# A hybrid diffusion backbone on one core: the framework's timeline simulation as the scheduling model of every engine's queue

## The chip, the core and the metric

The kernel runs on one core of one Trainium2 chip. A core has a matrix engine (TensorE, "PE" in the profile), a vector engine (VectorE, "DVE"), a scalar engine (ScalarE, "ACT"), a general engine (GpSimd, "POOL") and a queue engine that only issues transfers (SyncE, "SP"). Each takes its instructions from a queue of its own, in the order in which they stand there, and waits at the head of the queue until the semaphores that the instruction needs have come. TensorE writes to PSUM, eight banks; the other memory on the chip is SBUF. The metric is the device time of one execution in microseconds (us); smaller is better. A figure given for a kernel is the median of its runs.

## The reference

Two layers work on 256 context tokens and 512 latent tokens of width 1024. Each layer is a mixer and an MLP, both between norms and with modulation from a conditioning vector (adaLN). Cut to what matters:

```python
def token_mixer(h_lat, h_ctx, p, rope, layer_idx, ctx_out):
    a_l, b_l, c_l, d_l, gate_l = split_cols(h_lat @ p['w_in'], GROUP_COLS)
    a_x, b_x, c_x, d_x, gate_x = split_cols(h_ctx @ p['w_in'], GROUP_COLS)
    ya = diff_attention(a_l, a_x, ...)       # softmax minus lambda * softmax
    yb = rwkv7_time_mix(b_l, b_x, ...)       # a recurrence in both directions
    yc = retention(c_l, c_x, ...)            # decayed linear attention, both directions
    yd = window_gqa(d_l, d_x, ...)           # banded attention with sink logits
    m = sum(sigmoid(gate_n) * (y_n @ w_branch[n]) for the four branches)
    return m @ p['w_out']

def sq_relu_mlp(h, w_up, w_down):
    return jnp.square(jax.nn.relu(h @ w_up)) @ w_down
```

All of it is float32. The output is the latent stream after two layers, (1, 512, 1024).

## The kernel before

The kernel is written against a framework that takes a program of tiles and builds the engines' queues from it. `kernel` opens a `TileContext` (line 1825), and `Build.run` states the whole computation inside it, layer by layer. When the context closes, the framework orders every engine's queue, gives out the buffers of the pools, and adds the semaphores. To order the queues it walks a simulated machine: whenever an engine is free in it, the first instruction in the program's order whose inputs and buffers are ready there goes next into that engine's queue. So the final order follows the program's order, with exchanges between neighbours where the simulated machine has something later ready sooner. The framework has two such machines, and the kernel before uses its default one.

Products are made in pieces of 128 by 128 weights against 256 or 512 tokens. A product of full precision is three matmuls: `mm3` (line 398 issues them) multiplies the high part of one operand with the high and low parts of the other, and the low with the high. So each block of weights is loaded (`unit`, line 262, on SyncE's queue, into four raw buffers), cast to its high part (line 265, ScalarE, `wh`), and its low part is the difference (line 266, `wl`, on VectorE, or on GpSimd where `pool_split` says so), in four buffers of each. The activations are kept as `hh` and `hl`.

The stages of a layer, in the order of the program:

- `branch_b` (line 802), the recurrence, as blocks of 64 tokens. Its chain goes from engine to engine: a norm of the keys (`head_sums`, line 594; a power operation on GpSimd, line 856; `rb`, line 619, a copy on VectorE that spreads the result over columns; the transposes `prs`, line 625, on TensorE), gram matrices (`pgr`, line 1001, masked into `gb` and `gk` by VectorE), a triangular inverse of 31 steps of two VectorE operations (lines 1123 and 1125), then small products (`pq`, `pz`, `ppu`, `pst`).
- The rest of the mixer: `branch_a` (scores `pas`), `branch_c` (`pcy`), `branch_d`, with the rotation of queries and keys in `spill` (`prot`, line 483); `gates` and `lift`, which bring the branches together.
- The output projection (`pwo`), the residual and the norm (`norm_tile`; a power operation on GpSimd, line 358; `xn`, line 377; the transposes `pnt`, line 381).
- The MLP (`pm` for the hidden layer, `pd` for the output).

While a branch's chain has TensorE wait, other projections fill it. The program says so by hand: `fill` (line 452) takes a number of microseconds of matmuls from a list of generators (`filler`) and states them there. The numbers stand in the table `FILL` (line 27), two sets, one for each layer. The modulations of later norms (`ada_steps`, `pada`, line 291) are such fillers too.

## Time and profile before

| | us |
|---|---|
| median of three runs | 2775.91 |
| lowest and highest run | 2770.07 and 2776.38 |
| the profiled execution | 2782.34 |
| its span, first to last instruction | 2780.6 |

| engine | busy us | share of the span |
|---|---|---|
| PE | 2623.3 | 94% |
| DVE | 1492.3 | 54% |
| ACT | 1082.6 | 39% |
| POOL | 703.2 | 25% |

The profile is of one execution. Busy time counts the instructions at work; the matmuls of a queue overlap, so a busy PE needn't be at its peak. The granted clock is the share of TensorE's full clock in a stretch. A wait is idle time of an engine, put down to what came last before the engine went on. Times in a view are microseconds from the first instruction, unless marked ns.

### The profile page before, as it was taken

The page shows a single profiled execution, that of the slowest core. Times are in us where ns is not written, and L with a number is a line of the kernel's source. Part 1 is how long each engine was busy: PE and PEld are TensorE (multiplying, and loading weights), DVE is VectorE, ACT ScalarE, POOL GpSimd, SP SyncE. Part 2 cuts the span into 40 slices and gives each one's busy share as a digit, 9 for nine tenths or more (in the row PEclk, how much of TensorE's full clock was granted, in tenths as well). Part 3 has the DMA queues.
Part 4 walks back from the last instruction along what each step waited for, and adds up shares of the span by engine and source line. Part 5 has one row for each costly group of instructions (what it writes and reads, how often), then busy time and mean ns, then how long its engine had stood idle before and what let it go on. Part 6 is the DMA issues. An engine that isn't in the chain of part 4 may idle for free.

```text
span 2780.6 us, 44114 instructions
## 1 busy us (share of the span) xinstructions
PE 2623.3 (94%) x17093; PEld 2095.9 (75%) x17093; DVE 1492.3 (54%) x2521; ACT 1082.6 (39%) x2144; POOL 703.2 (25%) x774
## 2 busy tenths in 40 slices
PE   7899899999999999999999988989999999999998
PEld 4766677887788778887888776667788686778886
DVE  5676752775745452333334569585385864433444
ACT  4432442563446333222223344244364463333332
POOL 2434342113330321101101344353322422201011
PEclk9999999999999999999999989899999999999999
DMA  6133545444433522322222222354644536342322
GB/s 237 58 117 106 170 154 161 120 126 156 157 122 109 168 92 93 108 91 90 86 94 86 93 67 73 105 194 159 189 130 153 185 106 201 116 135 95 95 95 91
DMA packets 177777, 346.51 MB, mean 125 GB/s; under 512 B 19440, under 2 KB 33312, under 8 KB 177568
## 3 DMA queue, kind: packets, MB, share of 16 engines
q1 hardware_dynamic: 139680, 279.99, 31.0%
q10 hardware_dynamic: 30208, 44.97, 4.6%
q0 software_dynamic: 7680, 18.75, 2.6%
q8 instruction: 134, 2.20, 0.3%
q14 instruction: 75, 0.61, 0.1%
HBM read 280.55 MB, written 63.08 MB: 124 GB/s over the span
## 4 chain that ended last, share of the span: by engine, by line
PE 72%; DVE 13%; DMA 4%; ACT 4%; issue 4%; POOL 4%; SPq 0%; ACTq 0%; DVEq 0%; POOLq 0%
PE pm L398 39%; PE pd L398 14%; PE pwo L398 4%; PE plift L398 2%; PE pada L291 1%; DVE xm L1125 1%; DVE tmp L1123 1%; PE pas L1335 1%; PE pay L579 1%; DVE cpl L557 1%; DMA wr<-w_in 1%; DMA wr<-w_out 1%; PE pq L1158 1%; PE pst L1236 1%; POOL wl L266 1%
## 5 line engine op out<-in xcount | busy, mean ns | idle before, releaser
L398 PE MATMUL pm<-hh,wh 128*128 128x512 f32 (+1 forms) x2272 | 832.3, 366 | 9.4 <-ACT wh L265 3.9
L398 PE MATMUL pm<-hh,wl 128*128 128x512 f32 (+1 forms) x2272 | 822.0, 362 | 11.4 <-POOL wl L266 11.1
L398 PE MATMUL pm<-hl,wh 128*128 128x512 f32 (+1 forms) x2272 | 820.7, 361 | 0.5 <-DVE hl L393 0.4
L265 ACT CAST wh<-wr 128x512 fp32r<-128x512 f32 x516 | 317.9, 619 | 687.7 <-PE pm L398 281.6
L266 DVE TENSOR_TENSOR wl<-wr,wh 128x512 fp32r<-128x512 f32 x364 | 261.7, 722 | 498.5 <-ACT wh L265 477.6
L398 PEld LDWEIGHTS pm<-hh,wh 128*128 128x128 f32 x2272 | 438.4, 193 | 97.3 <-issue 25.1
L398 PEld LDWEIGHTS pm<-hh,wl 128*128 128x128 f32 x2272 | 438.4, 193 | 79.5 <-POOL wl L266 13.1
L398 PEld LDWEIGHTS pm<-hl,wh 128*128 128x128 f32 x2272 | 438.7, 193 | 68.9 <-issue 8.8
L266 POOL TENSOR_TENSOR wl<-wr,wh 128x512 fp32r<-128x512 f32 x152 | 210.3, 1387 | 424.2 <-ACT wh L265 392.3
L1738 POOL TENSOR_TENSOR s<-r 128x256 f32<-128x256 f32 (+1 forms) x98 | 91.3, 931 | 758.8 <-ACT r L1737 754.4
L398 PE MATMUL pd<-wh,sh 128*128 128x512 f32 x640 | 254.6, 399 | 3.2 <-DVE hf L385 2.4
L398 PE MATMUL pd<-wh,sl 128*128 128x512 f32 x640 | 252.6, 396 | 1.1 <-DVE sl L1740 1.0
L398 PE MATMUL pd<-wl,sh 128*128 128x512 f32 x640 | 253.3, 396 | 0.0
L1740 DVE TENSOR_TENSOR sl<-s,sh 128x256 fp32r<-128x256 f32 (+1 forms) x98 | 58.0, 592 | 177.4 <-POOL s L1738 177.4
L398 PEld LDWEIGHTS pd<-wh,sh 128*128 128x128 f32 x640 | 120.7, 189 | 37.7 <-DVE hf L385 3.1
L398 PEld LDWEIGHTS pd<-wh,sl 128*128 128x128 f32 x640 | 120.6, 188 | 30.6 <-DVE sl L1740 1.9
L398 PEld LDWEIGHTS pd<-wl,sh 128*128 128x128 f32 x640 | 120.7, 189 | 28.3 <-DVE wl L266 0.2
L1784 DVE TENSOR_TENSOR acc<-acc,pd 128x512 f32<-128x512 f32 x120 | 82.4, 686 | 50.5 <-PE pd L398 49.4
L1525 POOL TENSOR_TENSOR merged<-merged,gateb 128x256 f32<-128x256 f32 (+1 forms) x72 | 88.3, 1232 | 78.3 <-DVE gateb L1524 77.6
L1737 ACT ACTIVATE r<-pm 128x256 f32<-128x256 f32 (+1 forms) x98 | 50.6, 516 | 118.7 <-PE pm L398 118.6
L398 PE MATMUL plift<-yh,wh 128*128 128x256 f32 (+1 forms) x192 | 73.3, 382 | 9.2 <-DVE gateb L1524 3.7
L1339 ACT ACTIVATE ae<-pas,asum 128x768 f32<-128x768 f32 (+1 forms) x80 | 65.2, 818 | 34.0 <-DVE asum L1337 31.4
(388 smaller groups left out, 3990.0 us busy)
## 6 DMA issues: line engine op xcount, KB each, us to landing
wr<-w_in SPq DMA_DIRECT2D x228, 256.0 KB
wr<-ada SPq DMA_DIRECT2D x192, 256.0 KB
wr<-w_up SPq DMA_DIRECT2D x128, 256.0 KB
wr<-w_down SPq DMA_DIRECT2D x128, 256.0 KB
graw<-gate ACTq DMA_DIRECT2D x64, 256.0 KB
x<-x SPq DMA_DIRECT2D x28, 512.0 KB
gateb<-graw SPq DMA_DIRECT2D x32, 384.0 KB
wr<-w_br SPq DMA_DIRECT2D x32, 256.0 KB
```

The source lines that it names most:

```text
L265: nc.scalar.copy(hi, raw)
L266: (nc.gpsimd if self.pool_split > h else nc.vector).tensor_tensor(lo, raw, f32(hi), ALU.subtract)
L291: nc.tensor.matmul(ps[32 * j:32 * j + 32, 0:256], self.silu[:, k, :], raw[:, i * 256:(i + 1) * 256], start=k % kn == 0, stop=k % kn == kn ...
L398: self.nc.tensor.matmul(ps, a[u], b[v], start=start and i == 0, stop=stop and i == 2)
L557: self.nc.vector.tensor_tensor(lo, src, f32(hi), ALU.subtract)
L579: self.nc.tensor.matmul(py, v.rearrange("p e d -> p (e d)"), w[i], start=start and i == 0, stop=stop and i == 1)
L1339: nc.scalar.activation(e[:, 0:nkc], ps[:, 0:nkc], ACTF.Exp, bias=sums[:, c:c + 1], accum_out=sums[:, 2 + c:3 + c])
L1525: nc.gpsimd.tensor_tensor(mo, mo, t, ALU.add)
L1737: nc.scalar.activation(r[:, 0:n], ps[:, 0:n], ACTF.Relu)
L1738: nc.gpsimd.tensor_tensor(s2[:, 0:n], r[:, 0:n], r[:, 0:n], ALU.mult)
L1740: nc.vector.tensor_tensor(s[1][:, o:o + n], s2[:, 0:n], f32(s[0][:, o:o + n]), ALU.subtract)
L1784: nc.vector.tensor_tensor(a, a, po[t - t0], ALU.add)
```

## The change

The `TileContext` is opened with the flag that makes the framework walk its other machine, the timeline simulation, when it orders the queues. The program that is stated inside the context is the same, and so are the engine, the operands and the pools of every instruction, and the `FILL` numbers. All five queues are ordered anew, SyncE's loads among them, and so the semaphores differ too.

```diff
     out = nc.dram_tensor("out", (SEQ, D), F32, kind="ExternalOutput").ap()
-    with tile.TileContext(nc) as tc:
+    with tile.TileContext(nc, schedule_with_timeline_sim=True) as tc:
         Build(tc, aps, out).run()
```

## Rows read from the trace of the kernel before

**Rows 1.** The page's first part: busy us, share of the span, instructions of each engine.
```profile
PE 2623.3 (94%) x17093; PEld 2095.9 (75%) x17093; DVE 1492.3 (54%) x2521; ACT 1082.6 (39%) x2144; POOL 703.2 (25%) x774
```

**Rows 2.** Busy us by stage, columns named in the first line; the last three: clock, DMA.
```profile
core 0: us, PE busy (x) PEld busy (x) DVE busy (x) ACT busy (x) POOL busy (x), PEclk, DMA share, GB/s
0.00:70.00 70.00, 51.48 (x315) 34.71 (x316) 37.35 (x103) 33.91 (x71) 16.66 (x49) 0.95 0.67 235
70.00:420.00 350.00, 317.41 (x3511) 240.64 (x3510) 237.07 (x397) 133.21 (x258) 142.23 (x137) 0.95 0.36 121
...
1050.00:1540.00 490.00, 489.57 (x2534) 397.57 (x2533) 165.01 (x257) 133.17 (x247) 49.74 (x56) 1.00 0.29 92
...
1610.00:1960.00 350.00, 315.28 (x3326) 236.45 (x3325) 244.33 (x402) 137.29 (x262) 145.49 (x134) 0.92 0.35 117
...
2450.00:2730.00 280.00, 279.54 (x1218) 222.57 (x1217) 119.70 (x178) 92.10 (x154) 25.12 (x24) 1.00 0.33 107
2730.00:2781.00 51.00, 38.76 (x166) 30.53 (x164) 23.05 (x28) 13.40 (x25) 9.11 (x14) 0.90 0.21 72
```

**Rows 3.** TensorE's waits: who waited for whom, total us, times, longest us.
```profile
PE pm L398 <- POOL wl L266: 11.1, 8, 3.3
PE pnt L381 <- DVE xn L377: 9.5, 7, 3.3
PE pgr L1001 <- DVE gk L1025: 8.6, 7, 2.1
PE prs L625 <- DVE rb L619: 8.3, 4, 3.3
PE prot L483 <- ACT st L522: 7.9, 3, 4.0
...
PE pada L291 <- DMA wr<-ada: 6.9, 5, 4.2
PE pcy L579 <- DVE cpl L557: 5.5, 9, 1.9
...
PE pq L1158 <- DVE xz L1139: 4.4, 1, 4.4
...
PE pgr L1001 <- DVE gb L1008: 3.9, 9, 1.7
...
PE pwo L398 <- ACT hh L1529: 3.1, 3, 1.6
```

**Rows 4.** Order of time around 80 us: start, us, engine, line, what, [idle before].
```profile
80.17 2.28 POOL L856 TENSOR_TENSOR krs<-krs,mhalf 128x12 f32<-128x12 f32 x1 [1.62 <-DVE krs L855]
...
80.45 0.40 PE L398 MATMUL pm<-hh,wh 128*128 128x512 f32 x1
82.44 1.25 POOL L266 TENSOR_TENSOR wl<-wr,wh 128x512 fp32r<-128x512 f32 x1
82.49 1.62 DVE L619 COPY rb<-krs 128x768 f32<-128x768 f32 x1 [2.40 <-POOL krs L856]
...
84.16 1.12 PE L625 MATMUL prs<-idn,rb 128*128 128x128 f32 x6 [3.31 <-DVE rb L619]
...
84.94 0.77 PE L398 MATMUL pm<-hl,wh 128*128 128x512 f32 x1
```

**Rows 5.** Order of time around 1880 us, TensorE's instructions beside its wait there.
```profile
1879.77 0.40 PE L398 MATMUL pm<-hh,wh 128*128 128x512 f32 x1
...
1884.57 1.45 PE L1158 MATMUL pq<-xz,gb 32*32 32x32 f32 x24 [4.41 <-DVE xz L1139]
1885.96 0.80 PE L398 MATMUL pm<-hl,wh 128*128 128x512 f32 x1
```

**Rows 6.** Order of time around 206 us: the copy `rb` with GpSimd at rest.
```profile
205.81 0.56 DVE L619 COPY rb<-krs 128x768 f32<-128x768 f32 x1 [2.40 <-POOL krs L856]
```

**Rows 7.** Rows 2, tile `wl` alone: length, PE, PEld, DVE, POOL.
```profile
70.00:420.00 350.00, 99.44 (x270) 54.19 (x270) 0.69 (x1) 47.19 (x33) 0.95 0.36 121
1610.00:1960.00 350.00, 96.08 (x248) 51.43 (x249) 0.68 (x1) 54.93 (x38) 0.92 0.35 117
```

**Rows 8.** SyncE's queue: what its loads of weights waited for, same columns as rows 3.
```profile
SPq L262 <- POOL wl L266: 445.3, 103, 15.3
```

## The prediction, made before the change was built

> **What bounds the kernel now.** I read the page's busy line first: TensorE is at work for 2623.3 us of the span of 2780.6 us, so at most 157.3 us of the span are times in which it runs no matmul [rows 1]. Next comes the view of the stages. Two long stages, the inner parts of the two MLPs, have practically no idle time on TensorE: 489.57 of 490 us and 279.54 of 280 us, at a granted clock of 1.00 [rows 2]. No order can gain there. The head of the kernel has 18.5 us of idle time (70.00 - 51.48) and the end 12.2 us (51.00 - 38.76); the head waits for first loads and the end is the last residual chain, and neither has other work to pull in [rows 2]. What is left is 157.3 - 18.5 - 0.4 - 0.5 - 12.2 = 125.7 us, which lie in the two mixers, the output projections and the norms. The two stages of the recurrent branch have 32.6 us (350 - 317.41) and 34.7 us (350 - 315.28) of them, and there the granted clock is 0.95 and 0.92 on average, a mix of its two levels, 1.2 and 2.4 GHz [rows 2].
>
> The third view is the list of TensorE's waits, grouped by what ended last. Ten entries hold 68.7 us (11.1 + 9.5 + 8.6 + 8.3 + 7.9 + 6.9 + 5.5 + 4.4 + 3.9 + 3.1), no single wait in them longer than 4.4 us [rows 3]. So there is no one big stall; there are some dozens of 1 to 4 us. The fourth view is the order of time around two of them, and it tells what an order can do about it. At 80.85 us TensorE stands for 3.31 us at the transposes `prs`, because GpSimd's power operation took 2.28 us and VectorE's copy `rb` behind it 1.62 us. The matmul that TensorE ran just before (80.45, `pm<-hh,wh`) and the one that it ran just after (84.94, `pm<-hl,wh`) are neighbours in one projection, and their operands were there all the time [rows 4]. The second case is the same: 4.41 us at `pq`, with members of a projection on both sides [rows 5]. In these places the queue's order is at fault and not a lack of work. The order was fixed before the run, by a model in which the wait was shorter than on the chip.
>
> **The change part by part.** It adds and removes no instruction of the computation; engine, operands, buffers and the order in which the program states the work stay. The framework builds each engine's queue by walking a simulated machine: when an engine is free in it, the first instruction in the program's order whose inputs and buffers are ready is put next. What changes is the machine that says what is ready when. The framework's source has prices for single GpSimd operations (the power operation among them) that only the timeline simulation uses; how right they are no row of the trace before can tell. So I cost places, not instructions: each wait of [rows 3] by what stands behind it in TensorE's queue.
>
> *Step 1, behind GpSimd's power operation:* `prs` behind `rb`, 8.3 us in four waits [rows 3]. Ready projection matmuls stand behind at least the longest one [rows 4]. If they go first, each wait is left with what one matmul overshoots, about 0.3 us: gain 8.3 - 4 x 0.3 = 7 us. Bounds: 0 (order unchanged) and 8.3.
>
> *Step 2, weights that GpSimd splits:* `pm` behind `wl`, 11.1 us in eight waits [rows 3]. The next matmuls add into the same PSUM bank, so only another projection could step in, and mostly one is under way at a time. Bounds 0 and 11.1; I take 4, nearer to nothing.
>
> *Step 3, the norm's transposes:* `pnt` behind `xn`, 9.5 us in seven waits [rows 3]. They stand where the next stage needs exactly this; I take 2 of 9.5.
>
> *Step 4, the recurrent branch and the rotation:* `pgr` 8.6 + 3.9, `prot` 7.9 and `pq` 4.4 us [rows 3]. For `pq` a ready matmul is shown [rows 5]: 4 us. Of the other 20.4 us I take a third, 7. Bounds 0 and 24.8.
>
> *Step 5, attention and output:* `pcy` 5.5 and `pwo` 3.1 [rows 3]: a quarter, 2 us.
>
> *Step 6, the loads.* SyncE's queue is built anew too, and it is a queue in order: a load put at its head before its buffer is free holds all loads behind it. Loads waited there for GpSimd's weight splits 103 times, up to 15.3 us [rows 8], and yet TensorE's waits that end with a load of `ada` come to 6.9 us [rows 3]. The bounds are therefore a gain of 6.9 us and a loss of about 15 for one badly placed load; I take 0, since the four raw-weight buffers and four split ones cover the ordinary case. If that cover goes, the 15 us are paid.
>
> *Step 7, new stalls.* Other waits of the 125.7 us, 57.0 us outside the ten entries, are short ones which the present order happens to pass quickly. A new order meets them differently; I charge a tenth, 6 us. Bounds: 0, and all that is gained.
>
> *The two dense stages* I cost at nothing: TensorE's matmuls there are fed with weights split well ahead, and the cover is that lead; if a new order breaks it, the first loss shows as idle time where there is now 0.4 and 0.5 us [rows 2].
>
> The sum: 7 + 4 + 2 + 11 + 2 - 6 = 20 us. The clock is left out of it: the recurrent stages grant 0.95 and 0.92, which is 0.05 x 350 + 0.08 x 350 = 45 us of full-clock time not granted [rows 2]; stalls that are filled may win back part of that, so it only widens the lower end. The profiled execution took 2782.34 us (span 2780.6 and 1.7 around it), 6.4 over the median of 2775.91. So: 2782.3 - 20 - 6.4 = 2756 us.
>
> **A row against the change.** The copy `rb` took 1.62 us at 82.49 us, started 0.05 us after GpSimd's 1.25 us weight split [rows 4]; the same copy with GpSimd at rest took 0.56 us [rows 6]. Beside GpSimd, VectorE's step was 1.06 us longer, and that lay in a wait of TensorE. The Trainium skill, page "SBUF — State Buffer", section "Summary: rules for kernel authors", states that when VectorE is in its two-port mode or has two SBUF inputs while GpSimd reads SBUF, the second to issue blocks entirely until the first is done. The trace agrees: the copy ended 0.42 us after GpSimd's end. By that rule a model which prices each engine alone would not see this wait, and the new order could be wrong at the same places or at new ones; it is the mechanism of the second rival, priced there from rows.
>
> **The rivals.** *No difference (chance 0.22).* The moves are local, the dependencies allow few others, and a stall filled early takes work that would have filled a later one; gains and losses of steps 1 to 7 cancel. That the flag alters next to nothing on the chip belongs here too. For it: TensorE is busy for 94% of the span [rows 1], and the stages with idle time have it in small pieces. Against it: two shown places with ready work behind a stall [rows 4, 5]. Time: 2776 us, the present median.
>
> *Slower, through collisions of VectorE and GpSimd (0.30).* The recurrent branch's chain runs on VectorE, and the stages that hold it run 33 and 38 weight splits on GpSimd, 71 in all, together 102 us [rows 7]. If the new order starts these splits as soon as the simulated machine has their inputs, more of them fall beside VectorE's chain. One costs 1.06 us as above [rows 4, 6]. The point from which it decides is 20 / 1.06 = 19 more collisions on the chain than now, about a quarter of the 71: that eats up the sum. With two thirds of them, 47, the loss is 47 x 1.06 = 50 us against a gain of 20: 2776 + 30 = 2806 us. Speaking for it is that VectorE is at work for 237 and 244 of 350 us in these stages [rows 2], so that a split finds it busy more often than not; against it, that the splits are as many as before and many collide already.
>
> *Faster, as summed (0.48).* 2756 us; its own range is 2720 to 2767.
>
> **How the numbers follow.** About 0.3%, 8.3 us, is what a measurement of this kernel can tell from no change. Faster by more than that, under 2767.6, takes the forecast's 0.48; within it 0.22; slower, above 2784.2, 0.30. The lower end takes the upper bounds of steps 1, 2 and 4 (8.3 + 11.1 + 24.8 = 44.2, which is 22 more than the 22 counted for them) and half of the 45 us of clock: 2756 - 22 - 22 = 2712. The upper end is the slower rival with one misplaced load, 2806 + 15 = 2821. So 2712 to 2821, with a tenth left out on each side; both signs lie in it because neither is excluded by a row.
>
> **What the profile after would show.** Step 1: in TensorE's waits `prs` behind `rb` falls from 8.3 to about 1 us, and projection matmuls lie between the power operation and the transposes. Step 4: the wait at `pq` disappears. Steps 2 and 3: `wl` and `xn` stay above half their present size. The sum as a whole: TensorE's idle time falls from 157 to about 137 us. Dense stages: still under 1 us idle. Step 6 is wrong if waits ending with a load rise by more than 7 us. The slower rival would show VectorE's mean times in the recurrent stages up (its busy time there over 260 us each) with GpSimd's count unchanged. The prediction is wrong at its root if the ten entries are as large as now or larger: then the new model is no nearer to the chip where it matters, or has traded one error for another. The other way to be wrong is idle time falling while the time doesn't, because the granted clock in the recurrent stages went down.

## The result, and the profile after

The changed kernel is slower: 2803.66 us as the median of four runs (2800.57 to 2813.74) against 2776.14 for the kernel before measured beside it (2770.07 to 2784.94). The ratio is 1.0101, 95% interval 1.0073 to 1.0128. The profiled execution took 2813.74 us with a span of 2811.8; the one before had 2780.6, so the two traces differ by 31.2 us, a little more than the medians.

The busy line of the changed kernel's page, beside [rows 1]:

```profile
PE 2651.3 (94%) x17093; PEld 2122.3 (75%) x17093; DVE 1485.2 (53%) x2521; ACT 1091.9 (39%) x2144; POOL 715.3 (25%) x774
```

The same 17,093 records of TensorE take 28.0 us longer, and its idle time is 160.5 us where it was 157.3. So new idle time explains only a tenth of the loss. TensorE's mean granted clock is 0.966 over the span, against 0.973 before. Worked out as in the prediction, 0.034 x 2811.8 = 95.6 us of full-clock time were not granted, against 0.027 x 2780.6 = 75.1: 20.5 us more. That can account for at most 20.5 of the 28.0 us of busy time; what the other 7.5 us are, no view shows.

The stages show where. Here are both kernels cut at the same events: layer 0 from its start to the last matmul of the gate `pgt` at the end of the recurrent branch, then the rest of the mixer up to the first `pwo` (called the attention stage from here on), and the same two for layer 1. First the kernel before, then the changed one; columns as in [rows 2].

```profile
0.00:420.00 420.00, 368.90 (x3825) 275.35 (x3826) 274.42 (x500) 167.12 (x329) 158.88 (x186) 0.95 0.41 140
420.00:929.40 509.40, 490.72 (x2901) 420.70 (x2900) 281.12 (x547) 242.52 (x527) 122.17 (x135) 1.00 0.45 139
...
1596.60:1953.20 356.60, 318.87 (x3334) 239.12 (x3334) 250.07 (x409) 140.77 (x271) 147.38 (x138) 0.91 0.36 121
1953.20:2335.00 381.80, 364.47 (x1822) 296.04 (x1822) 232.71 (x400) 196.05 (x395) 106.21 (x111) 0.98 0.52 159
```
```profile
0.00:479.20 479.20, 442.48 (x4181) 335.15 (x4182) 275.81 (x512) 185.49 (x361) 174.23 (x196) 0.95 0.42 140
479.20:933.00 453.80, 430.37 (x2543) 372.43 (x2542) 268.18 (x535) 225.79 (x495) 111.76 (x125) 0.98 0.45 137
...
1602.60:2011.00 408.40, 373.01 (x3559) 278.73 (x3557) 263.11 (x428) 159.09 (x303) 157.96 (x148) 0.94 0.39 129
2011.00:2370.10 359.10, 324.38 (x1595) 265.13 (x1595) 219.11 (x386) 181.91 (x365) 95.42 (x101) 0.94 0.47 144
```

Both recurrences are longer, by 59.2 and 51.8 us, and both attention stages are shorter. Layer 0 gets 55.6 us back in its attention stage, layer 1 only 22.7. With the output projection and the MLP, layer 0 ends 6.0 us late (1602.6 against 1596.6) and layer 1 adds 25.2. The counts say why the stages moved: 356 matmuls changed sides in layer 0 (3825 to 4181) and 225 in layer 1 (3334 to 3559). Nearly all of the 225 are projections that are now done during the recurrence: of the records of `pm` in layer 1's attention stage, 993 before, 770 are left. The recurrence of layer 1 has 54.1 us more busy time with them, and its idle time is only 2.3 us less (37.7 to 35.4), so they hardly filled its waits. In layer 0's recurrence idle time did fall with the 356, by 14.4 us (51.1 to 36.7). Layer 1's attention stage has the 225 no more: its idle time went from 17.3 to 34.7 us and its granted clock from 0.98 to 0.94.

Projections that depend on no chain can be run at any time and so can fill any wait; the text calls them the stock. Four stretches of that stage, 104.7 us long together, hold most of its idle time (columns as above):

```profile
2126.60:2156.50 29.90, 21.11 (x116) 18.43 (x117) 19.13 (x40) 13.15 (x30) 6.41 (x10) 0.77 0.44 132
2216.40:2231.30 14.90, 9.63 (x39) 7.83 (x38) 4.32 (x9) 4.54 (x8) 6.33 (x9) 0.77 0.81 248
2291.20:2336.10 44.90, 35.83 (x181) 28.52 (x180) 23.41 (x54) 27.07 (x60) 1.51 (x1) 0.81 0.19 60
2351.00:2366.00 15.00, 9.50 (x36) 7.28 (x35) 7.97 (x10) 6.83 (x14) 3.88 (x3) 0.87 0.61 199
```

They hold 28.6 of the stage's 34.7 us of idle time, and 0.23 x 29.9 + 0.23 x 14.9 + 0.19 x 44.9 + 0.13 x 15.0 = 20.8 us of clock not granted. The whole stage lacks 0.06 x 359.1 = 21.5 us of clock, so the rest of it was granted nearly all. Projections (`pm`) fill 29.47 us of these 104.7, 28%; in the rest of the stage they fill 160.65 of 254.4 us, 63%. Over the whole stage they fill 190.12 of 359.1 us, 53%, where they filled 240.08 of 381.8 us, 63%, in the kernel before. TensorE's waits in the first and third stretch are 1 to 2 us at the most, for exponentials and splits (`ae`, `de`, `wtl`, `yraw`); the second and the fourth hold one each of over 5 us, for a transfer and for the gate.

TensorE's waits, beside [rows 3]:

```profile
PE pvc L1045 <- DVE gk L1025: 10.4, 5, 3.2
PE pada L336 <- DMA wr<-ada: 8.5, 5, 4.4
PE pnt L381 <- DVE xn L377: 7.5, 2, 5.5
PE pas L1335 <- ACT ae L1339: 7.2, 8, 1.5
PE pnz L1098 <- ACT kt L1088: 7.2, 2, 4.6
PE pdw L1461 <- DVE yraw L585: 6.1, 8, 1.1
```

The entries of [rows 3] that are left stand further down the same list (lines between them left out):

```profile
PE pgr L1001 <- DVE gb L1008: 4.5, 3, 3.2
PE pwo L398 <- ACT hh L1529: 3.3, 5, 1.1
PE pcy L579 <- DVE cpl L557: 2.9, 5, 1.1
PE pgr L1001 <- DVE gk L1025: 2.2, 2, 1.6
PE pm L398 <- POOL wl L266: 1.2, 1, 1.2
PE prot L483 <- ACT st L522: 0.8, 1, 0.8
PE pada L291 <- DMA wr<-ada: 0.5, 1, 0.5
```

`prs` behind `rb` and `pq` behind `xz` are gone, `prot` fell from 7.9 to 0.8 us, `pm` behind `wl` from 11.1 to 1.2. The wait at `gk` has only moved: `pgr` behind it fell from 8.6 to 2.2 us, but `pvc`, which had no wait, now stands behind the same `gk` for 10.4. The ten entries of [rows 3] sum to 69.2 us; in the changed kernel they sum to 22.9 (7.5 for `pnt` and the seven lines above). All other idle time of TensorE rose from 157.3 - 69.2 = 88.1 to 160.5 - 22.9 = 137.6 us, by 49.5. Among the new waits are those of the attention steps: `pas` behind `ae` was 1.4 us before, `pdw` behind `yraw` 0.7.

One more view differs. VectorE's step of the recurrent chain, `sn`, waits for the chain's matmul `pst`; the kernel before first, then the changed one (us in total, times):

```profile
  PE pst L1236: 20.7, 39
```
```profile
  PE pst L1236: 93.0, 33
```

A chain has ten hops from `pst` over `sn` to the next `pst`. From the first `pst` to the end of the last one, the four chains took 14.0, 15.3, 15.4 and 13.0 us and now take 35.1, 37.5, 31.6 and 36.2. In TensorE's queue, 1 to 9 matmuls stood between two hops; now up to 27 do. One such gap in the changed kernel, TensorE's instructions in order of time and then VectorE's step:

```profile
1800.82 0.48 PE L398 MATMUL pm<-hh,wh 128*128 128x512 f32 x1
...
1803.22 0.40 PE L398 MATMUL pm<-hl,wh 128*128 128x512 f32 x1
1803.45 0.40 PE L398 MATMUL pm<-hh,wl 128*128 128x512 f32 x1
1803.78 0.33 PE L1248 MATMUL po<-gb,x 128*64 128x64 f32 x2
1804.04 0.45 PE L1236 MATMUL pst<-sn,big 64*64 64x64 f32 x8
```
```profile
1799.24 0.59 DVE L1239 TENSOR_TENSOR sn<-sn,pst 64x128 f32<-64x128 f32 x2
...
1804.52 0.60 DVE L1239 TENSOR_TENSOR sn<-sn,pst 64x128 f32<-64x128 f32 x2 [3.18 <-PE pst L1236]
```

Nine more `pm` lie where the dots are. The `sn` that the hop takes in was ready at 1799.83 us; the hop's matmuls ran at 1804.04, behind a projection, and VectorE was idle for 3.18 us.

### The profile page after: what moved, and what is told of

Same layout as the page of the kernel before. It is cut to its first block, busy times and chain, and to the rows that moved or that the text cites. A ratio compares the mean times of both kernels' runs of the same rounds, so it can differ in the third digit from the quotient of the medians.

```text
span 2811.8 us, 44150 instructions
## 1 busy us (share of the span) xinstructions
PE 2651.3 (94%) x17093; PEld 2122.3 (75%) x17093; DVE 1485.2 (53%) x2521; ACT 1091.9 (39%) x2144; POOL 715.3 (25%) x774
## 5 line engine op out<-in xcount | busy, mean ns | idle before, releaser
L398 PE MATMUL pm<-hh,wl 128*128 128x512 f32 (+1 forms) x2272 | 813.7, 358 | 1.2 <-POOL wl L266 1.2
L398 PE MATMUL pd<-wh,sh 128*128 128x512 f32 x640 | 248.9, 399 | 2.7 <-ACT hf L389 2.0
L1337 DVE TENSOR_REDUCE asum<-pas 128x1 f32<-128x768 f32 (+1 forms) x80 | 67.5, 847 | 36.6 <-PE pas L1335 32.5
```

The costliest lines, as they stand in the source:

```text
L398: self.nc.tensor.matmul(ps, a[u], b[v], start=start and i == 0, stop=stop and i == 2)
L1337: nc.vector.tensor_reduce(sums[:, c:c + 1], ps[:, 0:nkc], AX.X, ALU.max, negate=True)
```

## The experiments

A word on the source, since several experiments turn on it. The timeline simulation gives each engine a simulated issue window: instructions are handed over ahead of their turn until the window is full, and what has been handed over keeps its place. TensorE's window is 35 deep, the others' 12. Theory A, formed from the view of the hops: a windowful of ready projections is handed over before a chain's next step becomes ready, so each step waits behind them, and TensorE's order carries the loss. Rival B: the loss comes from the order of the other queues.

Where TensorE's order is held below, this function does it; the list of numbers comes from another kernel's queue, and the other engines are ordered by the scheduling model around it. (`KINDS` names the matmul instructions, `unpack` makes the list out of a string; a line that only compares lengths is left out at the dots.)

```diff
+def pin(tc, engine, order):
+    ins = [i for i in tc.nc.cur_bb.bb.instructions if i.engine == engine and type(i).__name__ in KINDS]
...
+    for a, b in zip(order, order[1:]):
+        tc.add_manual_dep(ins[b], ins[a].name, mybir.DependencyInfo(mybir.DependencyClass.NoSync, mybir.DependencyReason.DATA),
+                          reason="order")
```

**e1: the changed kernel with TensorE in the order of the kernel before.**

```diff
         Build(tc, aps, out).run()
+        pin(tc, mybir.EngineType.PE, unpack(PE_ORDER))
```

> Timeline simulation for all five queues, but TensorE's queue is held to the exact order that it had in the kernel before. Theory A (the loss is in TensorE's own order: about 20 matmuls of other work stand ahead of each step of the recurrence's chain, and attention in the second layer lacks them later): the loss goes, 2765 to 2785 us, against 2803.7 with the change whole. Theory B (the loss is in the order of the other four queues, VectorE and GpSimd colliding or loads misplaced): 2795 to 2810 us.

2786.78 us, ratio to the kernel before 1.0055 (1.0031 to 1.0078). That is just above theory A's range and below B's. Some half of the loss is gone. The other half shows that the order of the other queues matters too; it isn't the changed kernel's, since the model orders them around TensorE's (VectorE's queue differs from that of the changed kernel in 1,524 of 2,521 places, and from that of the kernel before in 932).

**e2: the kernel before with TensorE in the changed kernel's order**, the same lines with the other list, in the kernel before.

> The framework's default machine for all five queues, but TensorE's queue is held to the exact order that it has in the changed kernel. Theory A (TensorE's order): as slow as the changed kernel, 2795 to 2815 us. Theory B (the other queues' order): 2768 to 2784 us.

2829.17 us, ratio 1.0206 (1.0164 to 1.0248). TensorE's new order, with the other queues ordered around it by the first model, loses more than the whole change, more than either theory gave it. That agrees with A as far as the loss comes with TensorE's order. It isn't that order alone, though: VectorE's queue differs from that of the kernel before in 1,528 of 2,521 places. The timeline simulation's order of the other queues makes up for half.

**e3, e10, e4: smaller windows for TensorE** (2, 4 and 8), all else as in the changed kernel.

```diff
+    from concourse.hw_specs import TRN2Spec
+    TRN2Spec.ENG_ISSUE_QUEUE_DEPTH = {**TRN2Spec.ENG_ISSUE_QUEUE_DEPTH, mybir.EngineType.PE: 2}
     with tile.TileContext(nc, schedule_with_timeline_sim=True) as tc:
```

> Timeline simulation, with one number of its model changed: TensorE's issue window, the count of instructions that the simulated sequencer hands to the engine ahead of their turn, 2 in place of 35. In the queue that comes out, 3 to 7 matmuls stand between two steps of the recurrence's chain, in place of 20. Theory A in its narrower form (the order is fixed when the simulated sequencer hands an instruction over, so a ready projection of a whole window gets in front of each step): VectorE's waits for that chain fall from 93 to under 35 us, the second layer's attention has its work back, and the time is 2755 to 2780 us. Rival (the order of the chain doesn't matter, only how true the prices are): within 8 us of the changed kernel, 2795 to 2812.

> As the run with a window of 2, with 8. In the queue 7 to 10 matmuls stand between two steps of the chain, with short ones split off. Theory A: VectorE's waits for the chain between those of windows 2 and 35, 35 to 60 us, and the time between theirs, 2765 to 2790 us. Rival: 2795 to 2812 us.

> The changed kernel with TensorE's simulated issue window of 4: 3 to 9 matmuls between hops. Theory A: 2735 to 2750 us, between the windows of 2 (2734.9) and 8 (2759.4). Rival B (a step somewhere between 4 and 8 and not a slope): 2755 or more.

**e8: a window of 1**, and **e11: windows of 2 for all engines** (`{e: 2 for e in TRN2Spec.ENG_ISSUE_QUEUE_DEPTH}`).

> The changed kernel with TensorE's simulated issue window of 1 instead of 35: at most some 2 matmuls between hops. Theory A (what is fixed ahead of its turn is all that costs): 2728 to 2740 us, the same as the window of 2 (2734.9) or a little faster. Rival B (a window of 1 has lost what a little run-ahead is good for, since TensorE then stands for every short wait): 2745 to 2770.

> The changed kernel with the simulated issue windows of all engines at 2, where the window of 2 had TensorE's alone (the others at 12). Theory A (only TensorE has a stock of ready work long enough to be handed over ahead of a chain's step): 2728 to 2742 us, the same as the 2734.9 of TensorE's window alone. Rival B (VectorE's and ScalarE's run-ahead costs the chains as well): 2715 to 2727.

The kernels in one table. "Ahead" is how many of the 1,828 projection and modulation matmuls that layer 1 has up to its first `pwo` stand in TensorE's queue before the end of its recurrence; "hop wait" is the wait of `sn` for `pst` as above.

| kernel | matmuls between hops | hop wait, us | ahead | median, us | ratio to before |
|---|---|---|---|---|---|
| before | 1 to 9 | 20.7 | 837 | 2776 | 1 |
| window 1 (e8) | 1 to 4 | 22.9 | 837 | 3165.29 | 1.1371 (1.1337 to 1.1406) |
| window 2 (e3) | 2 to 10 | 20.1 | 837 | 2734.85 | 0.9867 (0.9833 to 0.9900) |
| window 4 (e10) | 3 to 9 | 28.5 | 837 | 2730.61 | 0.9837 (0.9815 to 0.9859) |
| window 8 (e4) | mostly 7 or 8 | 35.6 | 862 | 2759.41 | 0.9947 (0.9927 to 0.9966) |
| window 35 (the change) | 1 to 27 | 93.0 | 1060 | 2803.66 | 1.0101 (1.0073 to 1.0128) |
| all windows 2 (e11) | 3 to 10 | 24.4 | 837 | 2726.02 | 0.9826 (0.9797 to 0.9854) |

Windows of 2 and 4 beat both kernels, the one before by 1.3 and 1.6%. Theory A had the direction right and the size wrong: the windows of 2, 4 and 8 all came out under the ranges that it gave (2755 to 2780, 2735 to 2750 and 2765 to 2790), and 4 is level with 2 and not between 2 and 8. For the other engines' windows e11 has to be held against e3: it is 8.8 us faster, inside rival B's range and outside A's, but the intervals of the two ratios overlap, so whether those windows cost anything stays open. The window of 1 fell outside both expectations by far. Its order hardly departs from the program's own: 1,344 of 14,359 matmuls moved, against 4,724 in the window of 2. So hardly anything steps into TensorE's waits; its idle time is 427.8 us (3163.8 - 2736.0), and its mean granted clock is 0.928. Four of its waits:

```profile
PE pm L398 <- ACT gate L1495: 29.5, 8, 5.3
PE pnz L1098 <- ACT kt L1088: 28.5, 9, 11.3
PE pdy L579 <- DVE dwtl L557: 23.9, 15, 3.5
PE pgr L1001 <- DVE gk L1025: 23.4, 4, 5.9
```

**e5, e6: the changed kernel with TensorE's old order in one layer alone.** In the list only the matmuls of that layer are kept; the others are free (8608 is the first one of layer 1 in the program's order; e6 has `0 <= k < 8608`).

```diff
+    order = [k for k in order if 8608 <= k < 1000000]
     for a, b in zip(order, order[1:]):
```

> The changed kernel, with TensorE's matmuls of layer 1 alone held in the order of the kernel before (5,751 of 14,359, from the norm ahead of layer 1's projections on); layer 0's matmuls are ordered by the timeline simulation, with 7 to 27 of them between one hop of the recurrent chain and the next; in layer 1 they are 1 to 9 again. Theory A (a longer recurrence is paid only where the work that was pulled ahead is missed afterwards; layer 0 has enough of it, layer 1 has not): 2775 to 2790 us, so as fast as the kernel with the old order in both layers (2786.8) or faster, and layer 0's recurrence still ends at about 475 us. Rival B (each layer's lengthened recurrence costs about half): 2793 to 2800.

> The changed kernel, with TensorE's matmuls of layer 0 alone (8,608 of 14,359) held in the order of the kernel before; layer 1's are ordered by the timeline simulation, with 1 to 23 between one hop and the next, most over 12. Theory A: nothing to speak of is won, 2798 to 2810 us, although layer 0's recurrence ends some 50 us earlier. Rival B: half of what both layers together brought (17 us), 2793 to 2797.

e5: 2779.6 us, ratio 0.9998 (0.9978 to 1.0018). e6: 2811.61 us, ratio 1.01 (1.0062 to 1.0139). In e6 layer 0's recurrence ended at 428.0 us and not at 479.2, and nothing was won: MLP 0 ended at 1603.7 against 1602.6. (2811.61 us is a little above theory A's upper end.) In e5 the recurrence ended at 472.0, and layer 1 alone gave all the time back. **So the loss comes with TensorE's order in layer 1**, and a stage that gets longer is no loss in itself. The two layers differ in what is left: layer 0 has 1,443 projection and modulation matmuls for its attention stage, layer 1 only 768. One thing stays open: e5 is faster than e1, so with the old order in layer 1 the new order of layer 0 is worth 0.6%, while with the new order in layer 1 (e6) it is worth nothing. Of the 13.0 us between the spans of e1 and e5, only 4.2 lie in layer 0's two stages; 7.5 lie in layer 1's, where TensorE's order is the same in both.

**e9: only the hops.** In the changed kernel's own order, at most 6 foreign matmuls stay between two hops; the other 292 go directly behind the chain.

> The changed kernel with TensorE held to its own order, but for the four recurrent chains: of the matmuls that stand there between one hop and the next and do not belong to the chain (projections, modulation), 6 stay in a gap and the others go behind the chain, 292 matmuls of 14,359 in all; the chain's own products stay where they are, so gaps are 6 to 21 in place of 1 to 27. Theory A (the matmuls in front of the hops are what lengthens the recurrence, and with it the kernel): each chain falls from 31 to 37 us to 15 to 23 us, and the time to 2775 to 2795 us. Rival B (the chains are the sign, and other places of the order cost the time): chains shorten and the time stays at 2797 to 2810.

2805.66 us, ratio 1.0104 (1.0077 to 1.0131). The chains did shorten, to 19.1, 17.9, 19.3 and 17.5 us, and the hop wait fell from 93.0 to 37.7 us:

```profile
  PE pst L1238: 37.7, 35
```

The time did not move. **Theory A falls here in its first form.** The delayed hops were a sign and not the cause: the last `pgt` of layer 1 started at 2007.2 us against 2010.4, since the matmuls moved out of the gaps were still ahead of it. That gave theory C: what costs is how many projections are used up by the end of layer 1's recurrence, wherever in it they stand.

**e12: the changed kernel with those 225 matmuls held back** to where the kernel before has them, with the old order behind the recurrence. The edit is a list: the changed kernel's order up to the last `pgt` of layer 1 without the 225, then the rest in the order of before.

> The changed kernel with TensorE held to its own order up to the end of layer 1's recurrence, but for 225 matmuls (223 of projections, 2 of a rotation) that it does there and the kernel before did only in the attention stage; these are held back to the places that they had in the kernel before, and the rest of the program follows the kernel before. The gaps of 20 and more between the hops stay in the first of layer 1's two chains and go in the second. Theory C (the cost is the projections used up before the attention stage, wherever they stand in the recurrence): 2775 to 2792 us, close to the 2779.6 of the whole of layer 1 in the old order; layer 1's attention and output stage has its idle time back under 25 us. Rival D (the fine order within the recurrence costs it): 2797 to 2812.

**e13: the fast kernel of window 4 with layer 1's recurrence in the changed kernel's order**, and so with the 225 ahead.

> The kernel with TensorE's window of 4 (2730.6 us) held to its own order, but for layer 1's recurrence, which has the changed kernel's order and with it 225 matmuls more than before (the attention stage after it has 225 fewer, in the order of the window of 4). Theory C: 2750 to 2765 us. Rival D' (the other places of the order let the loss grow, and without them it is nothing): 2728 to 2742.

e12: 2790.09 us, ratio 1.0061 (1.0037 to 1.0084), within C's bounds, but near their upper end; the attention stage's idle time is 21.7 us (17.3 in the kernel before, 34.7 in the changed one). e13: 2753.96 us, ratio 0.9924 (0.9899 to 0.9949), 23 us over e10, as C expected. But e13 changes two things at once: the 225 matmuls come with the changed kernel's fine order of that recurrence, so its 23 us are the price of both. The two stages of layer 1 in e10 and then in e13:

```profile
1569.40:1913.20 343.80, 310.25 (x3333) 231.25 (x3331) 248.52 (x409) 141.41 (x272) 147.34 (x138) 0.94 0.38 125
1913.20:2288.50 375.30, 361.59 (x1822) 296.58 (x1821) 232.82 (x403) 199.08 (x397) 108.72 (x111) 0.98 0.53 163
```
```profile
1573.30:1984.80 411.50, 375.84 (x3558) 281.55 (x3556) 262.68 (x427) 158.91 (x303) 158.68 (x148) 0.93 0.39 129
1984.80:2311.60 326.80, 308.31 (x1595) 253.56 (x1596) 220.53 (x385) 181.57 (x365) 94.97 (x101) 0.98 0.51 157
```

The recurrence is 67.7 us longer and the attention stage 48.5 us shorter, a net loss of 19.2 us. Idle time is a small part of it: 33.6 to 35.7 us in the recurrence, where the 225 fill hardly anything, and 13.7 to 18.5 in the attention stage. The larger part is that the one stage has 65.6 us more of busy time and the other 53.3 less. Of these 12.3 us, 8 go with the clock in these two executions: 0.06 x 343.8 = 20.6 us not granted in e10's recurrence, 0.07 x 411.5 = 28.8 in e13's. With 768 projections left, e13's attention stage is still granted 0.98 and has 18.5 us of idle time, where the changed kernel with the same 768 has 0.94 and 34.7. So the count alone did not make the changed kernel's attention stage so thin; its own order there has a part in it.

**Theory C is shown only for a part of the loss.** e12 got back some 40% of it, with the 225 held back and the attention stage in the old order; e5 got back all. Layer 1's recurrence in e12 and then in e5:

```profile
1597.10:1964.50 367.40, 326.83 (x3332) 246.03 (x3331) 247.11 (x410) 142.02 (x272) 146.97 (x139) 0.91 0.37 118
1598.20:1949.60 351.40, 310.10 (x3334) 234.35 (x3332) 255.69 (x410) 140.39 (x271) 148.60 (x138) 0.94 0.37 122
```

With nearly the same number of matmuls, e12 takes 16.0 us longer; the larger part of the loss, some 60%, goes with the fine order within this recurrence and the other queues ordered around it. How it costs the time is not settled. 12.0 us of the difference are clock not granted (0.09 x 367.4 = 33.1 and 0.06 x 351.4 = 21.1), but the kernel before has e5's order of TensorE there and was granted 0.91 as well, in 356.6 us, and e1, again with that order, 0.93; so the clock of one execution can't be laid to the order. The table of the windows, too, speaks against the count as the only cause: the window of 8 has only 25 matmuls more ahead than the window of 4 and is 29 us slower, and 19.8 us of the difference between their spans lie in layer 0's two stages (420.3 and 512.8 us against 414.7 and 498.6). No run here changes the count alone.

**e7: the window of 2 with a cheap power operation in the price list.**

```diff
+    TRN2Spec.GPSIMD_OP_FIXED_NS_AND_CYCLES_PER_ELEMENT = {**TRN2Spec.GPSIMD_OP_FIXED_NS_AND_CYCLES_PER_ELEMENT, "Pow": (93, 2)}
```

> The kernel with TensorE's simulated issue window of 2, in whose price list GpSimd's power operation is cut to the price of a multiply, as the first scheduling model takes it; all else is the same. Theory A (what makes the window of 2 faster than the kernel before is that the timeline simulation knows GpSimd's slow operations and places what waits for them later): 2755 to 2780 us, with TensorE's wait for the norm's statistics (rb or rs) back at 5 us or more. Rival B (that price is one of many, and the gain is spread over all waits): 2732 to 2748, with that wait under 3 us.

2742.58 us, ratio 0.9849 (0.9818 to 0.9881), inside B's range, with an interval that overlaps with that of e3. The wait of `prs` for `rb` came back with 3.7 us, a little over the 3 that B allowed. The one price is not what makes the window of 2 fast; that the gain is spread over all waits, as B said, fits this but isn't shown by it.

**e14: the kernel before with TensorE in the order of window 4.** The same two lines as in e2 with that list.

> The kernel before, with the first scheduling model on all engines, and TensorE's matmuls held in the order of the window of 4. If the gain of the small window (some 45 us against the kernel before) lies in TensorE's order: 2725 to 2745 us. If it lies in the order of the other queues, or needs both: 2760 to 2790.

2757.84 us, ratio 0.9938 (0.9915 to 0.9961): under the second expectation, short of the first. TensorE's order carries some 17 of the 45 us that the window of 4 gains; the rest needs the other queues ordered with it. All six pairs together, as ratios to the kernel before:

| TensorE's order of | others by the first model | others by the timeline simulation |
|---|---|---|
| before | 1 | 1.0055 (e1) |
| the change | 1.0206 (e2) | 1.0101 |
| window 4 | 0.9938 (e14) | 0.9837 (e10) |

In each column TensorE's order from the change is the slowest and that of the window of 4 the fastest. Across, the simulation's order of the other queues is worth 1% where TensorE's order is its own, and costs 0.55% where it is a foreign one. The other queues are ordered anew around TensorE's in each pair, so no pair changes one queue alone.

## Why the prediction was wrong

The likeliest case was 2756 us, faster; it came out 2804, inside the range and on the other side.

**Steps 1 to 5 had the gains right in kind and took them too small.** The waits at `prs`, `pq`, `prot` and `wl` fell, `wl` by 9.9 us where step 2 took 4 and had it stay above half its size, `xn` by 2.0 as step 3 took, `pcy` by 2.6. Step 4 was wrong for `gk`, whose wait moved to `pvc` (8.6 us before, 2.2 and 10.4 after). The ten entries, which the prediction adds up to 68.7 us, sum to 69.2; they fell by 46.3 us, where steps 1 to 6 counted 26. A new order by the timeline simulation can gain: e10, where the stock stays where it was, gained some 45 us. But that came only partly through the entries named: in e10 `prs` fell to 1.5 and the 4.4 us at `pq` are gone, but `wl` (9.7) and `gk` (8.4) stand. Its idle time on TensorE is 126.5 us (2729.2 - 2602.66) where it was 157.3, spread over all stages, and its granted clock 0.977, which leaves 62.8 us not granted where it was 75.1.

**Step 7 is the step that failed.** It took new stalls as a tenth of the short waits, 6 us, with all that is gained as the upper bound. Idle time outside the ten entries rose by 49.5 us, more than the 46.3 that the entries lost, so idle time rose by 3.2 us where the sum had it fall by 20. The step treats each wait by itself, as if filling one took nothing from another. The rival of no difference had the right thought in one clause, that a stall filled early takes work that would have filled a later one, and priced it at a tie. In layer 1 it was worse than a tie: 225 matmuls were moved into a stage where they hardly filled anything (idle 37.7 to 35.4 us) and out of one whose idle time then doubled (17.3 to 34.7). Holding them back, with the attention stage in its old order, brought back some 40% of the loss (e12). The rest goes with the fine order in layer 1's recurrence; how that order costs the time stays open. Bounding this step by the stock would have given a warning: 837 of layer 1's 1,828 matmuls ahead left 991 for the attention stage, and nothing in the sum limits how many a model may take ahead.

**The moves are local: wrong.** This was said for the rival of no difference. The old queue holds each matmul within 78 places of the program's order; in the changed one the furthest has moved 557.

**The clock is the second term that failed.** It was left out of the sum, with the note that it only widens the lower end. It worked upwards: 20.5 of the 31.2 us between the traces go with it. The last sentence of the prediction looked for it in the wrong place: the recurrent stages were granted 0.95 and 0.94, no less than before, and the attention stages lost it.

**The slower rival came near in time, 2806 us, by a mechanism that did not occur.** Its sign was to be VectorE's busy time over 260 us in each recurrent stage. In the windows of [rows 2] it was 237.07 and 244.33 us and is now 221.00 and 238.32, though these windows no longer hold the same work. Cut at the events, layer 1's recurrence has 263.11 us, where it had 250.07, but for 428 instructions and not 409: 0.61 us for one both times. Over the whole kernel VectorE's 2,521 instructions took 1485.2 us where they took 1492.3, and the copies `rb` met fewer splits (below).

**Steps 5, 6 and the dense stages.** `pwo` behind `hh` stayed (3.1 to 3.3 us). Loads did not become late: the two entries of `ada` sum to 9.0 us (8.5 and 0.5) and summed to 11.5 before, the 6.9 of [rows 3] and this line, which the prediction did not count:

```profile
PE pada L336 <- DMA wr<-ada: 4.6, 1, 4.6
```

The dense stages kept their cover: the last MLP's stage took 339.4 us against 340.2.

## What to carry to other kernels

Work that can be done at any time is a stock: before a schedule is changed, count per stage how much of it is used up and how much the later stages with short waits still need; here a stage in which it filled hardly anything only got longer. A scheduler that hands work over ahead of its turn can spend that stock early (1060 matmuls ahead with the window of 35, 837 with 1, 2 and 4), so the depth of its run-ahead is the first thing to vary (1, 2, 4, 8 and 35 gave 3165, 2735, 2731, 2759 and 2804 us). The count is not the whole of an order: of the loss some 60% went with the fine order of one stage, and of the gain of the window of 4 some 60% needs the other queues ordered with it. And a symptom in the trace, however large (93.0 us of hop wait), is a cause only once its removal has moved the time.

## What the runs showed of the hardware

In the four stretches above TensorE was idle for 20 to 37% of the time and was granted 0.77 to 0.87, a mix of its two levels, 1.2 and 2.4 GHz, while the rest of the stage was granted nearly all. So beside 28.6 us of idle time, 20.8 us of clock were not granted there. Idle time does not tell the granted clock by itself: layer 1's recurrence was granted 0.91 with 37.7 us of it (before) and 0.94 with 41.3 (e5), in the same order of TensorE's matmuls.

The blocking of VectorE by GpSimd went with the order of the work. The four copies `rb` of `krs` took 1620 ns as the median in the kernel before and 562 in the changed one, with the same operands:

```profile
L619 DVE COPY rb<-krs x4: 561/1620/1624, 82.5 to 1766.4; 128x768 f32<-128x768 f32 x4
```
```profile
L619 DVE COPY rb<-krs x4: 536/562/958, 83.0 to 1766.0; 128x768 f32<-128x768 f32 x4
```

In the changed kernel GpSimd ran no split beside the first of them: its next one started at 84.13 us, and the copy ran from 82.97 for 0.56 us, where before it ran 1.62 us beside a split [rows 4]. Beside the third one a split did run, but it began 0.01 us after the copy and not before it:

```profile
1653.83 0.56 DVE L619 COPY rb<-krs 128x768 f32<-128x768 f32 x1 [1.59 <-POOL krs L856]
1653.84 1.70 POOL L266 TENSOR_TENSOR wl<-wr,wh 128x512 fp32r<-128x512 f32 x1
```

Here the copy kept its 0.56 us and the split took 1.70 us, where the one in [rows 4], which began first, took 1.25. The Trainium skill, page "SBUF — State Buffer", section "Summary: rules for kernel authors", states that when VectorE is in its two-port mode, or has two SBUF inputs while GpSimd reads SBUF, the second of the two to issue blocks until the first is done. The trace agrees in all three places: the one that began second was the long one, and the copy without a neighbour was short. That the copy ran in the two-port mode, no row shows. As a rival, the collisions had the wrong sign: of the four copies, three began within 0.1 us behind a GpSimd split before and took 1.62 us each; in the changed kernel one began behind a split, by 0.20 us, and took 0.96 us.
